# Attention stage: the low part of each weight block by ScalarE's negative high part and an adding transfer, in place of a VectorE subtraction

## The chip, the core and the metric

The kernel runs on one core of a Trainium2 chip. Its engines are TensorE (PE in the profile, PEld for its weight loads), VectorE (DVE), ScalarE (ACT), GpSimd (POOL) and SyncE (SP, which here only starts transfers). Each engine works through its own list of instructions in order, and waits where an instruction's input is not ready. The metric is the device time of one execution in microseconds; of several runs the median is taken.

## The reference, cut to what matters

Two layers over 256 image tokens ("lat") and 256 context tokens ("ctx") of width 1024. Each layer is a half feed-forward, a mixer, and another half feed-forward, each followed by a layer norm. The mixer of the first layer is attention, the only place that the change touches:

```python
def proj(xs):
    p = xs @ w_in                       # 1024 -> 1536 columns
    q, k, v = jnp.split(p, [ATT_HEADS * ATT_HEAD_DIM, (ATT_HEADS + ATT_KV_HEADS) * ATT_HEAD_DIM], axis=-1)
    q = rms_norm(q.reshape(B, L, ATT_HEADS, ATT_HEAD_DIM), q_gain)
    k = rms_norm(k.reshape(B, L, ATT_KV_HEADS, ATT_HEAD_DIM), k_gain)
    ...
s = jnp.einsum('bqhgd,bkhd->bhgqk', q, k).astype(jnp.float32) * (ATT_HEAD_DIM ** -0.5)
p = jax.nn.softmax(s, axis=-1).astype(v.dtype)
...
o_lat = jnp.moveaxis(ob, 0, 1).reshape(B, L, D_MODEL) @ w_out     # 1024 -> 1024
```

Image queries (8 heads) look at all 512 keys, context queries at the 256 context keys; keys and values have 2 heads; image queries and keys are rotated (rope). The mixer's output, times a gate, is added to the residual and normalized.

## The kernel before

**Products in three.** All large products run on TensorE in a rounded float32 type (F32R). To keep float32 accuracy, each operand is held as two tiles: a high part `h` (the value rounded to F32R) and a low part `l` (the value minus `h`). A product is three matmuls into one accumulator, high x high, high x low, low x high (`mm3`, lines 211, 214, 215; `token_product`, lines 726 to 728, where the tokens are the stationary side).

**Weight blocks.** Weights come as blocks of 128 x 1024 float32 (512 KB). `raw` (line 173) takes one of 3 buffers of the tag "raw" and starts the load on SP (line 179). `pair` (line 182) takes one of 7 buffers of the tag "w", which hold a high and a low part. `chunk` (line 187) does both and calls `split`, which makes the parts: ScalarE writes the high part (line 194), VectorE subtracts it from the raw block and writes the low part (line 199). Where `self.fine` is set, as it is throughout attention, VectorE does this in four quarters of 256 columns, so that TensorE can begin with the first; otherwise in one piece. Only when VectorE is done is the raw buffer free for the next load. `split` is also used for everything else that needs two parts: activations, queries, keys, values, probabilities.

`Stream` asks `chunk` for a block when the program first uses it and holds the last block alone; `Keep` holds all its blocks. Buffers of one tag are given out in the order of the program; an instruction that writes a new tile waits until an old tile's last reader has finished.

**Order of the work.** The program is traced in Python order, and a planner then writes each engine's list when the program is built: of what is ready by its own estimates, the instruction that stands first in the program. `pin` keeps some instructions in program order. [...]

**The stage.** `attention` follows the first half feed-forward, whose last products and whose layer norm (`norm`, lines 380 to 480, one generator per token group, advanced by `steps`) still run when it begins. It has these parts:

- `part(blk, tt)`: the input projection, 6 column blocks of 256, each of two weight blocks (12 in all, held with `Keep`), times 4 token tiles of 128. Blocks 0 to 2 for the image tokens, then for the context tokens, then block 3 for all; blocks 4 and 5 follow, partly between the heads.
- `evac` and `turn`: the rms norm of queries and keys (sum of squares on ScalarE, line 782; reciprocal root on VectorE, lines 223 to 234; scaling, line 789), the rotation on GpSimd (lines 752 to 758), and transposes on TensorE (line 797).
- `scores` and `values`: for each head and each of three row blocks the scores, the softmax (lines 820 to 833, one of the three scalings on GpSimd), transposes (line 840), the split of the probabilities, and the product with the values. The probabilities' parts take a buffer of the tag "w" per head.
- `mix_unit`: the output projection, one unit per 128 columns; `w0` (4 weight blocks, `Stream`) for the first four heads, beginning between the last heads' work, then `w1` (4 weight blocks) for the others, first for image tokens, then for context tokens. The sums go on VectorE (line 715).

GpSimd has in this stage the rotation, a third of the softmax scalings, and some sums and differences of the layer norm (lines 417 and 454). It starts no transfers in the kernel before. After the stage the second half feed-forward's weights come through the same "raw" and "w" buffers.

Of the kernel before, what the change touches and what calls it, by code (L numbers as in the profile page):

```python
# [13 lines left out]
AF = mybir.ActivationFunctionType  # L14
ALU = mybir.AluOpType
# [96 lines left out]
class Stream:  # L112


    def __init__(self, b, chunks, sh=0):
        self.b, self.chunks, self.kept = b, chunks, (None, None)
        self.sh = sh if callable(sh) else lambda c: sh
# [24 lines left out]
class Body:  # L142
    def __init__(self, ctx, tc, a, out):
        self.tc, self.nc, self.a, self.out = tc, tc.nc, a, out
        self.n = 0
        self.sp = ctx.enter_context(tc.tile_pool(name="sp", bufs=1))
        self.pp = ctx.enter_context(tc.tile_pool(name="pp", bufs=1, space=PSUM))
        self.later, self.running = [], []
        self.fence = {}
        self.fine = False  # L150

        self.nraw, self.spare = 0, None

# [33 lines left out]
    def chunk(self, src, sh=0):  # L187
        r = self.raw(src)
        h, l = self.pair(sh=sh)
        self.split(r, h, l)  # L190
        return h, l

    def split(self, x, h, l):
# [537 lines left out]
    def attention(self, gate, side):  # L731
        nc, V, S, a = self.nc, self.nc.vector, self.nc.scalar, self.a
        with self.tc.tile_pool(name="att", bufs=1) as gp:
# [131 lines left out]
                    kept.append(hd)  # L865

            wait, kept = [], []

            def turns(left):
                while len(wait) > left:  # L870
                    turn(*wait.pop(0))
# [48 lines left out]
            for gr in both:  # L920
                for d in range(ND - MTAIL, ND):
                    self.mix_unit(g, both, d, w1, gr, d * 4, range(4, 8), True, MTAILSTEP)
            self.steps(ENDSTEP)


    def mlstm(self, gate, side):
# [472 lines left out]
```

## Time and profile before

| What | Value |
|---|---|
| Median of 3 runs | 1699.26 us (1698.13 to 1702.44) |
| Span of the profiled execution | 1693.6 us; the profile gives no time of that execution beside its span |
| Median above the span | 5.7 us |
| Busy, TensorE / VectorE / ScalarE / GpSimd | 1643.8 / 1231.7 / 656.3 / 93.6 us |
| Granted TensorE clock, mean | 0.994 |
| Attention, roughly | 374 to 564 us of the span |

The span is the time from the first to the last instruction of the program in one profiled execution. A row of a group of instructions gives its line, engine and operation, what it writes and reads (buffer numbers left out), its shapes and count, then its busy time and the mean of one in ns, then the idle time of the engine just before these instructions and what ended most of it. A row of a timeline gives start and duration in us, then engine and line; "x4" means that four of a kind are merged, and the brackets give an idle time before it and what ended it. A row of waits reads: who waited, for whom, us in total, times, longest. DVE L199 is the subtraction of `split`, whoever called it.

### The profile page before, as it was taken

To read this page: it belongs to the slowest core of one execution; us is meant where nothing else is said; L and a number is where in the kernel's file an instruction comes from. 1 tells how busy PE (TensorE), PEld (TensorE's weight loads), DVE (VectorE), ACT (ScalarE), POOL (GpSimd) and SP (SyncE) were. 2 spreads that over 40 slices of the span, in tenths; PEclk is the share of its full clock that TensorE was granted. 3 is DMA by queue.
4 is the path that set the end of the run, shared out by engine and by line. 5 is a ranking of instruction groups with operands and counts; after the bars stand their busy time and mean duration, and the time that the engine had idled before them with its cause. 6 is when DMAs were issued, how large, how long until landed. Compare 5 with 4: busy or idle time off the path is not lost.

```text
span 1693.6 us, 24765 instructions
## 1 busy us (share of the span) xinstructions
PE 1643.8 (97%) x9432; PEld 1441.6 (85%) x9432; DVE 1231.7 (73%) x2681; ACT 656.3 (39%) x1125; POOL 93.6 (6%) x114
## 2 busy tenths in 40 slices
PE   7999999999899999999999999999999999999997
PEld 6888888899887898888888998888889878999986
DVE  6799977659988899996334977643335967998687
ACT  5622133215465452212331543213322645556541
POOL 0000000002321100000000100000001001120000
PEclk9999999999999999999999999999999999999999
DMA  9576765412102346774222257642221232337542
GB/s 356 184 230 231 236 210 199 149 62 77 61 2 82 119 136 234 229 244 152 93 94 75 101 179 247 215 144 98 99 100 63 94 125 76 113 125 246 178 168 94
DMA packets 71910, 250.49 MB, mean 148 GB/s; under 512 B 7920, under 2 KB 10480, under 8 KB 71792
## 3 DMA queue, kind: packets, MB, share of 16 engines
q1 hardware_dynamic: 71072, 248.15, 43.1%
q8 instruction: 74, 1.21, 0.3%
q10 hardware_dynamic: 720, 0.76, 0.1%
q14 instruction: 44, 0.36, 0.1%
HBM read 247.83 MB, written 1.05 MB: 147 GB/s over the span
## 4 chain that ended last, share of the span: by engine, by line
PE 83%; DVE 11%; ACT 3%; DMA 2%; issue 1%; POOL 0%; ACTq 0%; DVEq 0%; SPq 0%
PE t L214 23%; PE t L215 23%; PE t L211 23%; PE t L668 4%; DVE t L199 3%; PE t L1165 2%; PE t L726 2%; PE t L728 2%; PE t L727 2%; ACT t L194 1%; PE t L380 1%; DVE t L473 1%; DVE t L400 1%; DVE t L475 1%; DVE t L1201 1%
## 5 line engine op out<-in xcount | busy, mean ns | idle before, releaser
L211 PE MATMUL t<-t,t 128*128 128x512 f32 (+2 forms) x2540 | 856.1, 339 | 10.1 <-ACT t L194 7.5
L214 PE MATMUL t<-t,t 128*128 128x512 f32 (+2 forms) x2540 | 858.5, 339 | 1.8 <-DVE t L475 1.3
L215 PE MATMUL t<-t,t 128*128 128x512 f32 (+2 forms) x2540 | 854.4, 337 | 1.9 <-DVE t L199 1.9
L199 DVE TENSOR_TENSOR t<-t,t 128x256 fp32r<-128x256 f32 (+2 forms) x793 | 494.8, 659 | 196.4 <-ACT t L194 195.8
L194 ACT CAST t<-t 128x1024 fp32r<-128x1024 f32 (+2 forms) x463 | 397.7, 880 | 587.0 <-PE t L215 311.2
L211 PEld LDWEIGHTS t<-t,t 128*128 128x128 f32 x2540 | 476.6, 188 | 65.7 <-ACT t L194 9.8
L214 PEld LDWEIGHTS t<-t,t 128*128 128x128 f32 x2540 | 477.7, 188 | 56.5 <-DVE t L475 2.5
L215 PEld LDWEIGHTS t<-t,t 128*128 128x128 f32 x2540 | 477.5, 188 | 55.3 <-DVE t L199 2.8
L290 DVE SCALAR_TENSOR_TENSOR t<-t,t 128x1024 bf16<-128x1024 f32 x224 | 262.6, 1220 | 15.9 <-DMA t<-in_ada_w 15.4
L522 DVE TENSOR_TENSOR t<-t,t 128x512 f32<-128x512 f32 (+1 forms) x93 | 54.0, 585 | 112.1 <-PE t L215 92.4
L521 ACT ACTIVATE t<-t 128x512 f32<-128x512 f32 (+1 forms) x93 | 47.4, 515 | 196.9 <-PE t L215 195.0
L417 POOL TENSOR_TENSOR t<-t,t 128x256 f32<-128x256 f32 x30 | 23.3, 777 | 1161.4 <-ACT t L407 1159.9
L557 DVE SCALAR_TENSOR_TENSOR t<-t,t,t 128x256 f32<-128x256 f32 x96 | 42.7, 478 | 54.2 <-PE t L215 54.2
L726 PE MATMUL t<-t,t 128*128 128x256 f32 (+1 forms) x256 | 80.4, 316 | 0.0
L728 PE MATMUL t<-t,t 128*128 128x256 f32 (+1 forms) x256 | 79.7, 314 | 0.0
L727 PE MATMUL t<-t,t 128*128 128x256 f32 (+1 forms) x256 | 79.5, 313 | 0.0
L1165 PE MATMUL t<-t,t 128*128 128x512 f32 (+1 forms) x248 | 54.8, 373 | 11.0 <-ACT t L274 5.2
L1165 PEld LDWEIGHTS t<-t,t 128*128 128x128 f32 x248 | 46.4, 220 | 19.0 <-ACT t L274 5.2
L668 PE MATMUL t<-t,t 128*128 128x512 f32 x264 | 60.0, 389 | 0.0
L668 PEld LDWEIGHTS t<-t,t 128*128 128x128 f32 x264 | 49.5, 188 | 10.2
L407 ACT ACTIVATE t<-t 128x256 f32<-128x256 f32 x72 | 26.1, 413 | 68.3 <-DVE t L400 68.3
L726 PEld LDWEIGHTS t<-t,t 128*128 128x128 f32 x256 | 49.6, 194 | 3.1 <-DVE t L789 0.3
(164 smaller groups left out, 1067.6 us busy)
## 6 DMA issues: line engine op xcount, KB each, us to landing
t<-in_ffn_in SPq DMA_DIRECT2D x168, 512.0 KB, 4.0
t<-in_ada_w SPq DMA_DIRECT2D x139, 512.0 KB, 4.2
t<-in_ffn_out SPq DMA_DIRECT2D x66, 512.0 KB, 3.7
t<-in_ffn_last SPq DMA_DIRECT2D x22, 512.0 KB, 3.7
t<-in_att_in SPq DMA_DIRECT2D x12, 512.0 KB, 3.5
t<-in_att_out SPq DMA_DIRECT2D x8, 512.0 KB, 3.9
t<-in_ml_qk SPq DMA_DIRECT2D x8, 512.0 KB, 3.4
t<-in_ml_v SPq DMA_DIRECT2D x8, 512.0 KB, 4.0
```

Source lines behind the costliest of these rows:

```text
L194: self.behind(self.nc.scalar.copy(h, x))
L199: self.behind(self.nc.vector.tensor_tensor(out=ls, in0=xs, in1=hs.bitcast(F32), op=ALU.subtract))
L211: ins = mm(out, wh, xh, start=first, stop=False)
L214: mm(out, wh, xl, start=False, stop=False)
L215: mm(out, wl, xh, start=False, stop=last)
L290: ins = nc.vector.scalar_tensor_tensor(self.tmp().bitcast(BF16), r, 1.0, self.cb[:, v, :], ALU.mult, ALU.mult, accum_out=to)
L522: V.tensor_tensor(out=sl, in0=sl, in1=pu[:, :n], op=ALU.mult)
L668: pin(nc.tensor.matmul(ys[tt][i], gs[g], ws[k][w][:, i * 512 : (i + 1) * 512], start=k == 0 and g == w == 0, stop=k == NF - 1 and g == 1,))
L726: mm(o, self.xh[:, k, c], wh, start=k == 0, stop=False)
L727: mm(o, self.xh[:, k, c], wl, start=False, stop=False)
L728: mm(o, self.xl[:, k, c], wh, start=False, stop=k == ND - 1)
L1165: mm = lambda *k, **kw: pin(nc.tensor.matmul(*k, **kw))
```

## The change

A flag `added`, off at first, is switched on in `attention` just before its first projection and off after its last step. While it is on, `chunk` makes the two parts in another way: ScalarE writes the high part as before, ScalarE then writes the negative of the rounded block into the low part's tile, and GpSimd starts a transfer from the raw block to the low part's tile that adds what it carries to what is there. The low part is then raw minus high, as before. VectorE has no part in it, and the four quarters become one transfer of 512 KB. It concerns 20 blocks: 12 of the input projection and 8 of the output projection. Splits of anything but weight blocks stay as they are, and so do all other stages.

```diff
         self.fine = False
+        self.added = False
...
     def chunk(self, src, sh=0):
         r = self.raw(src)
         h, l = self.pair(sh=sh)
-        self.split(r, h, l)
+        if self.added:
+            S = self.nc.scalar
+            self.behind(S.copy(h, r))
+            self.behind(S.activation(l, r, AF.Copy, scale=-1.0))
+            self.nc.gpsimd.dma_start(l, r, accum_op=ALU.add)
+        else:
+            self.split(r, h, l)
         return h, l
...
             wait, kept = [], []
+            self.added = True
...
             self.steps(ENDSTEP)
+            self.added = False
```

## The prediction

> **What bounds the kernel now.** I read the engines' totals first.
>
> ```profile
> PE 1643.8 (97%) x9432; PEld 1441.6 (85%) x9432; DVE 1231.7 (73%) x2681; ACT 656.3 (39%) x1125; POOL 93.6 (6%) x114
> ```
>
> TensorE (PE) is busy in 97% of the span, so a change pays only where PE stands still or is about to. Next the busy time of each engine in the three stretches of attention (columns: length; busy us and instructions of PE, PEld, DVE, ACT, POOL; granted clock; DMA share; GB/s): the projections, the softmax stretch, the output product.
>
> ```profile
> 374.00:436.00 62.00, 60.06 (x501) 59.13 (x499) 58.33 (x205) 34.78 (x88) 12.65 (x16) 1.00 0.28 91
> 436.00:513.00 77.00, 67.69 (x498) 62.97 (x497) 64.65 (x201) 42.60 (x141) 25.27 (x22) 0.93 0.03 9
> 513.00:553.00 40.00, 36.85 (x208) 31.09 (x207) 33.68 (x86) 20.93 (x40) 3.13 (x2) 1.00 0.32 107
> ```
>
> VectorE (DVE) is full in the first stretch, 58.3 of 62 us, yet PE lacks only 1.9 us there: VectorE is late, but seldom late enough to stop PE. ScalarE (ACT) and GpSimd (POOL) have room everywhere. Then the waits between 370 and 560 us (total us, times, longest), those of PE alone:
>
> ```profile
> PE t L211 <- ACT t L194: 7.5, 7, 2.0
> PE t L797 <- POOL t L758: 2.6, 1, 2.6
> PE t L215 <- DVE t L199: 1.9, 1, 1.9
> PE t L380 <- DVE t L357: 1.1, 1, 1.1
> PE t L380 <- DVE t L443: 0.9, 2, 0.6
> ```
>
> VectorE itself stops PE for 1.9 + 1.1 + 0.9 = 3.9 us in all of attention. The largest item is the high-part cast on ScalarE (line 194), and the edit leaves that cast where it is.
>
> **What is taken away.** Line 199, for the 20 weight blocks of attention (12 of the input projection, 8 of the output), four quarter blocks each:
>
> ```profile
> L199 DVE TENSOR_TENSOR t<-t,t 128x256 fp32r<-128x256 f32 x106 | 41.9, 431 | 8.1 <-ACT t L194 8.1
> L194 ACT CAST t<-t 128x1024 fp32r<-128x1024 f32 x25 | 26.0, 1048 | 28.4 <-PE t L215 19.0 <-DMA t<-in_att_out 3.3 <-PE t L797 3.3
> 535.63 3.43 ACT L194 CAST t<-t 128x512 fp32r<-128x512 f32 x4 [2.59 <-PE t L840]
> ```
>
> That is 80 of the 106 quarter subtractions between 340 and 560 us: 80 x 41.9/106 = 31.6 us of VectorE. What PE can gain from it is less. In the projections the queue on VectorE is long, which one block shows (start, us): its cast, its last quarter's subtraction, and the load that had waited for its raw buffer.
>
> ```profile
> 381.78 1.05 ACT L194 CAST t<-t 128x1024 fp32r<-128x1024 f32 x1 [1.78 <-PE t L215]
> 398.42 0.87 DVE L199 TENSOR_TENSOR t<-t,t 128x256 fp32r<-128x256 f32 x1
> 399.35 29.39 SPq L179 DMA_DIRECT2D t<-in_att_in  x6
> ```
>
> 17.5 us from cast to complete low part; a transfer will be quicker than that, and such loads start earlier. Blocks that VectorE serves at once will be some 5 us later than now, but a block of the projections waits in its buffer for the products of the blocks ahead of it; I price that at nothing, and at 5 us if that cover is gone. The gain is what VectorE's norm chain and sums hold up: 1.1 (line 357) + 0.9 (line 443) = 2.0 us. The 1.9 us before line 215 come from splitting queries, not weights, and the 2.6 us before line 797 from the rotation on GpSimd behind a chain of small VectorE operations; both stay. I count **-2.0 us**; bounds 0 and, with those two, -6.5.
>
> **What is put in.** Per block one more ScalarE pass and one transfer started by GpSimd. The pass has the cast's shape: 1.05 us alone, 0.95 behind another one (the row at 535.63 is a 128x512 cast of 0.59 us and three of 128x1024). 20 x 0.95 = 19 us of ScalarE, which is busy 34.8 of 62 and 20.9 of 40 us in the two stretches where blocks are made: it fits. The transfer, from SBUF to SBUF and adding, has no row here. The nearest:
>
> ```profile
> q1 hardware_dynamic: 71072, 248.15, 43.1%
> t<-in_att_out SPq DMA_DIRECT2D x8, 512.0 KB, 3.9
> t<-in_ml_qk SPq DMA_DIRECT2D x8, 512.0 KB, 3.4
> t<-in_ada_w SPq DMA_DIRECT2D x2, 512.0 KB, 8.7
> 520.42 0.33 SPq L179 DMA_DIRECT2D t<-in_att_out  x1
> L417 POOL TENSOR_TENSOR t<-t,t 128x256 f32<-128x256 f32 x30 | 23.3, 777 | 1161.4 <-ACT t L407 1159.9
> 523.24 1.57 POOL L833 TENSOR_SCALAR t<-t,t 128x512 f32<-128x512 f32 x1 [6.39 <-DVE t L827]
> ```
>
> A load of the same 512 KB lands after 3.9 us; of that, 0.431 x 1693.6 x 0.524/248.15 = 1.5 us is the engines' own time. Adding reads the old block as well, so I count one more such pass: 5.4 us (bounds 3.4, the quickest load, and 8.7, loads in a crowded queue). Starting it costs GpSimd between SP's 0.33 and its own longest operation, 1.57; I take 0.8, its usual one. So a low part is complete 0.95 + 0.8 + 5.4 = **7.15 us** after its cast ends (bounds 4.7 and 11.2).
>
> [...]
>
> **Where it hurts.** The output blocks are made just in time. Rows: for the first two blocks the ScalarE row whose second cast is the block's, for the third the ScalarE row at 535.63 above, then quarter subtractions and PE's first products with each.
>
> ```profile
> 514.69 1.52 ACT L194 CAST t<-t 128x512 fp32r<-128x512 f32 x2
> 518.87 1.09 DVE L199 TENSOR_TENSOR t<-t,t 128x256 fp32r<-128x256 f32 x3
> 519.72 0.39 PE L211 MATMUL t<-t,t 128*128 128x512 f32 x1
> 519.94 0.39 PE L214 MATMUL t<-t,t 128*128 128x512 f32 x1
> 522.85 1.52 ACT L194 CAST t<-t 128x512 fp32r<-128x512 f32 x2
> 526.55 0.40 PE L215 MATMUL t<-t,t 128*128 128x512 f32 x1
> 537.20 3.11 DVE L199 TENSOR_TENSOR t<-t,t 128x256 fp32r<-128x256 f32 x9 [0.25 <-ACT t L194]
> 537.22 0.50 PE L211 MATMUL t<-t,t 128*128 128x512 f32 x1 [1.62 <-ACT t L194]
> 537.79 0.40 PE L215 MATMUL t<-t,t 128*128 128x512 f32 x1
> ```
>
> Each of these casts follows at once on the cast of a head's probabilities (the 128x512 one in its row), and no row of ScalarE names a load that it waited for: the buffers of tag "w" are given out in program order, so a block isn't made sooner unless that head is. The first block's cast ends at 516.2; low part at 523.4; PE needs it at about 519.7: 3.7 us late. The second: 524.4 + 7.15 = 531.5 against 526.55: 5.0 late. The third: cast over by 537.2, so 544.35 against 537.8: 6.6 late. The delays add, because each later cast waits for PE's work behind the earlier stall: **15.3 us** with PE's order as it is (bounds 7.8 and 27.3). (For the third PE waits 1.62 us already.) The subtractions had also come in quarters, so PE could begin on the first; the transfer comes whole.
>
> A planner writes each engine's order when the program is built, and a block that is ready later will be set behind other work. What is there to set before it: the rest of the last two heads,
>
> ```profile
> 518.69 0.28 PE L214 MATMUL t<-t,t 128*128 128x256 f32 x1
> 518.80 0.28 PE L215 MATMUL t<-t,t 128*128 128x256 f32 x1
> 525.81 0.44 PE t L840 x4
> ```
>
> six groups of transposes (0.44 each, by the chain of waits), 2 x 18 products of the values (0.12 from start to start) and the last scores (three products of 512 columns at 0.22, six of 256 at 0.12): 2.6 + 4.3 + 1.4 = 8.3 us. So between 15.3 - 8.3 = 7.0 us and nothing remains (nothing, because heads done earlier also bring the second and third cast forward). I take **+5**, nearer the upper end, because the order is settled before the transfer's real time is known and PE can't change it.
>
> Who else waits: behind each transfer's start on GpSimd stand the rotation (lines 752 to 758) and the scaling of the softmax (line 833), and PE's transposes wait for these; a start that itself waits for ScalarE's second pass holds them up. GpSimd has 3.1 busy us in the last 40, so I add nothing. SP's loads wait for the raw buffer, now returned 7.15 us after the cast, not after 1.5: the third block's cast ends at 537.2, and the load that takes its raw buffer starts at 538.69. The next such load is on the chain of waits already:
>
> ```profile
> 538.69 0.33 SPq L179 DMA_DIRECT2D t<-in_att_out  x1
> 540.03 4.93 DMA t<-in_att_out
> 545.04 1.54 ACT t L194 x2
> ```
>
> That chain would move by 5.6 us; it runs beside the stall on the third block, and counts within the 5.
>
> **Sum.** -2.0 + 5 = +3.0 us. The span is 1693.6 us; the profile gives no separate time of its own execution, and the median of the runs stands 5.7 us above the span, which I carry over unchanged: 1699.3 + 3 = **1702 us**. About 0.3%, 5 us, is what a measurement of this kernel can tell from no change.
>
> **Rivals.** (1) *PE's order stays*: 15.3 - 2.0 = +13.3, **1713** (1705 to 1725 by the bounds). For it: the blocks are tied to the heads by the buffers, and PE works in order. Against: 8.3 us of other work stand ready. (2) *VectorE is what counts*: relieved of 31.6 us, it shortens the chains in front of lines 380, 797 and 215, 6.5 us together, and PE's slow clock in the second stretch (0.93 over 77 us is 5.4 us) halves because PE stops less: -9.2 at best; with 3 us of stall left, -6: **1693**. Place: the projections and the first scores; it decides if the idle time before lines 797 and 215 shrinks below half. Against: VectorE already idles there for ScalarE and GpSimd. (3) *Nothing moves*: the fill hides the latency and VectorE wasn't on the path: **1699**.
>
> [...]
>
> ```profile
> 442.64 1.11 DVE L233 TENSOR_TENSOR t<-t,t 128x4 f32<-128x4 f32 x1
> 444.18 0.16 DVE L233 TENSOR_TENSOR t<-t,t 128x4 f32<-128x4 f32 x1
> 442.47 1.26 POOL L758 TENSOR_TENSOR t<-t,t 128x512 f32<-128x512 f32 x1
> ```
>
> The same operation takes 1.11 us beside GpSimd's rotation and 0.16 us after it. Starts of transfers could do the same to VectorE or suffer it; 20 x 0.95 us, mostly off the path, is within rival 1's range. [...]
>
> **Chances.** Forecast 0.48 (own range 1697 to 1707), rival 1 0.23, rival 2 0.15, rival 3 0.14. Slower by over 0.3%: 0.23 + a third of the forecast, 0.39. Faster: most of rival 2 and a tail of the forecast, 0.17. Within: 0.44. The range runs from just above rival 2's 1693 to rival 1's 1713.
>
> **What would show it.** Right: idle PE before lines 215 between 515 and 560 us, released by a transfer, several us in all; the waits of line 380 on VectorE gone; VectorE some 30 us less busy; transfers that take 3.4 to 8.7 us from start to landing. Wrong: no PE wait on a transfer (then rival 3 or 2); a wait of line 797 that grew (starts in GpSimd's queue); a transfer over 8.7 us, which would also hold up the projections. An order that changed far from attention would upset the sum as a whole.

## The result, and the profile after

The changed kernel takes **1724.2 us** (median of four runs, 1721.9 to 1726.6) against 1698.7 us for the kernel before (four runs, 1698.1 to 1702.4): a ratio of **1.015, interval 1.0133 to 1.0166**. It is 25.5 us slower. The forecast was 1702, its range ended at 1713, so both were wrong, though "slower" held 0.39 of the chance.

The spans of the two profiled executions differ by more, 1723.3 against 1693.6 us: 29.7. The time of a run stands 1.7 to 2.1 us above its span wherever both are known, so the profiled execution of before took some 1695.6 us, about 3 us under its median, and that of after 1725.1, 0.9 us over. What the traces are made to explain is therefore 29.7 us, of which some 4 are chance. Below, a ratio is turned into us with 1698.7.

First the totals of the profile page after: the engines, the queue of GpSimd's transfers (packets, megabytes, share of the span), and the median time of one from issue to landing.

```profile
PE 1655.3 (96%) x9432; PEld 1450.7 (84%) x9432; DVE 1210.2 (70%) x2601; ACT 674.3 (39%) x1145; POOL 109.6 (6%) x134
q0 software_dynamic: 2880, 10.49, 3.3%
t<-t POOLq DMA_DIRECT2D x20, 512.0 KB, 5.3
```

The edit did what it says: 80 operations and 21.5 us fewer on VectorE (31.6 were counted; by the operations' own times the quarters are 32.2 less and all others together 5.2 more, and VectorE's operations overlap by 110.1 us in place of 115.6), 20 passes and 18 us more on ScalarE, 20 transfers of 5.3 us.

Where the time went is read from the busy time by stretch, cut so that both kernels have done nearly the same matmuls at each cut (columns: length; busy us and instructions of PE, PEld, DVE, ACT, POOL; granted clock; DMA share; GB/s). Before:

```profile
366.00:564.00 198.00, 183.50 (x1359) 171.78 (x1357) 169.07 (x521) 106.08 (x277) 42.66 (x42) 0.97 0.20 69
564.00:1694.00 1130.00, 1105.35 (x6464) 973.00 (x6464) 777.08 (x1676) 429.69 (x679) 50.77 (x68) 1.00 0.42 140
```

After:

```profile
366.00:590.00 224.00, 191.25 (x1363) 177.42 (x1362) 148.94 (x446) 122.35 (x296) 57.34 (x61) 0.94 0.42 106
590.00:1723.00 1133.00, 1109.63 (x6464) 976.95 (x6464) 777.12 (x1676) 430.51 (x679) 51.03 (x68) 0.99 0.43 140
```

Attention grew by 26.0 us, everything behind it, up to the ends of the spans, by 3.7 (1129.6 and 1133.3 us). In attention PE stood still for 198.00 - 183.50 = 14.5 us before and for 32.75 after: 18.25 us more. The other 7.75 us are PE busy for longer with some 1360 matmuls in both: the granted clock fell from 0.97 to 0.94, and 0.06 x 224 - 0.03 x 198 = 7.5 us. **So two thirds are stalls and one third is a slower clock.**

What the stalls wait for, between 370 and 600 us after (total us, times, longest):

```profile
ACT t L193 <- DMA t<-in_att_in: 12.2, 3, 7.3
PE t L387 <- DVE t L364: 9.2, 2, 5.2
ACT t L193 <- DMA t<-in_att_out: 8.5, 1, 8.5
PE t L222 <- DMA t<-t: 6.0, 3, 4.4
PE t L804 <- DVE t L240: 3.8, 1, 3.8
PEld t L804 <- POOL t L765: 3.9, 1, 3.9
PE t L222 <- DVE t L206: 2.7, 1, 2.7
PE t L804 <- DVE t L206: 2.0, 1, 2.0
```

(Line 193 is now the high-part cast, 194 ScalarE's second pass, 195 the transfer; other lines have moved down by 7, those from `split` on.) PE's waits for ScalarE's casts, lines 193 and 201, are left out: 8.3 us, 7.5 before. PE's wait for the transfers themselves, line 222, is 6.0 us. The larger part, 9.2 us before line 387 (2.0 before the change) and 5.8 before line 804 (2.6 before), names VectorE, which has less to do than before. The new rows beside them are ScalarE's: its cast waits 20.7 us for weights to arrive, where the row of line 194 before (in the prediction) has 3.3.

How a late load becomes a stall in the layer norm, from GpSimd's and SP's timelines and from the chain of waits of after:

```profile
381.89 0.86 POOL L195 DMA_DIRECT2D t<-t  x1 [3.40 <-PE t L222]
390.14 0.33 SPq L180 DMA_DIRECT2D t<-in_att_in  x1
390.14 5.12 DMA t<-in_att_in
...
395.34 1.04 ACT t L193
396.38 0.42 ACT t L481
...
396.83 0.49 DVE t L482
...
398.10 0.35 DVE t L364
...
398.49 1.24 PE t L387 x2
```

The transfer that starts at 381.89 lands at 390.08 (8.2 us, beside loads). Only then is its raw buffer free, and the load that had waited for it starts at 390.14; in the kernel before, the same load started at 381.74. ScalarE's next instruction is the cast of that block; it stands until 395.34, and behind it in ScalarE's list stands the norm's line 481, which had nothing to do with weights. VectorE and then PE wait for that one: PE stands from 393.31 to 398.49.

This isn't one unlucky block. Nine loads of the projections need a buffer that comes back, and after the change each of the nine starts 0.05 or 0.06 us after a transfer has landed. In the kernel before, six of them started 1.5 to 6.7 us after the end of the cast of the block that had held the buffer, and three, behind VectorE's long queue, 12.8 to 16.5 us after it; now all nine start 5.8 to 10.2 us after it.

The 5.8 us before line 804 come from the last block of the projections. Its load stands behind a transfer until 435.94 (428.41 before the change):

```profile
442.50 1.05 ACT L193 CAST t<-t 128x1024 fp32r<-128x1024 f32 x1 [7.27 <-DMA t<-in_att_in]
445.57 0.17 DVE L230 TENSOR_SCALAR t<-t 128x4 f32<-128x4 f32 x1 [10.38 <-ACT t L789]
449.25 1.26 POOL L759 TENSOR_TENSOR t<-t,t 128x512 f32<-128x512 f32 x1 [3.58 <-DVE t L796]
451.94 1.26 POOL L765 TENSOR_TENSOR t<-t,t 128x512 f32<-128x512 f32 x1
```

While ScalarE stands for that load, the queries' sums of squares (line 789) stand behind it in ScalarE's list. For them wait VectorE's reciprocal root (from line 230) and scaling (line 796), then GpSimd's rotation (lines 759 to 765), then PE's transposes, which start at 453.25. So PE's 3.8 us end with the rotation, as the row of its weight load (PEld) says; line 240 of VectorE only happened to end 0.02 us later. The other 2.0 us, at 446 us, end with VectorE's part of a split whose cast stands behind the same load on ScalarE.

At the end of attention the same happens through SP's list:

```profile
555.37 7.46 DMA t<-in_att_out
...
565.23 4.49 DMA t<-t
569.72 0.02 SPq L180
...
569.77 0.33 SPq L180
...
570.20 9.20 DMA t<-in_c
...
579.47 1.28 ACT L272
...
590.80 0.81 PE t L387 x2
```

A load of weights waits for the raw buffer until 569.72, and SP's next transfer (line 271, an operand of the modulation, 512 KB) waits behind it, takes 9.2 us among the bunched loads (a DMA share of 1.00 from 570 to 580 us, in a row further down), and holds ScalarE until 579.47 and, through the norm, PE until 590.80: 4.05 us of idle PE, 0.9 before. In the kernel before, SP issued the same transfer without such a wait, and it landed in 5 us (SP's and ScalarE's timelines; line 264 is now 271, 265 is 272):

```profile
548.36 0.80 SPq L264 DMA_DIRECT2D t<-in_c  x2
553.47 1.28 ACT L265 ACT_TABLE_LOAD   x1 [2.21 <-DMA t<-in_c]
```

### The profile page after: what moved, and what is told of

It is laid out like the page before. It is cut to its first block, busy times and chain, and to the rows that moved or that the text cites. A ratio compares the mean times of both kernels' runs of the same rounds, so it can differ in the third digit from the quotient of the medians.

```text
span 1723.3 us, 24768 instructions
## 1 busy us (share of the span) xinstructions
PE 1655.3 (96%) x9432; PEld 1450.7 (84%) x9432; DVE 1210.2 (70%) x2601; ACT 674.3 (39%) x1145; POOL 109.6 (6%) x134
## 4 chain that ended last, share of the span: by engine, by line
PE 79%; DVE 11%; DMA 4%; issue 3%; ACT 3%; POOL 0%; SPq 0%; ACTq 0%; DVEq 0%; POOLq 0%
PE t L221 22%; PE t L222 22%; PE t L218 22%; PE t L675 3%; DVE t L206 2%; PE t L1174 2%; PE t L733 1%; PE t L735 1%; PE t L734 1%; PE t L387 1%; ACT t L201 1%; DMA t<-t 1%; DVE t L480 1%; DVE t L407 1%; DVE t L482 1%
## 5 line engine op out<-in xcount | busy, mean ns | idle before, releaser
L206 DVE TENSOR_TENSOR t<-t,t 128x256 fp32r<-128x256 f32 (+2 forms) x713 | 463.3, 684 | 204.7 <-ACT t L201 203.9
L201 ACT CAST t<-t 128x1024 fp32r<-128x1024 f32 (+2 forms) x443 | 377.5, 873 | 573.0 <-PE t L222 292.6
L218 PEld LDWEIGHTS t<-t,t 128*128 128x128 f32 x2540 | 478.7, 189 | 67.1 <-ACT t L201 9.0
L222 PEld LDWEIGHTS t<-t,t 128*128 128x128 f32 x2540 | 480.1, 189 | 63.0 <-DMA t<-t 7.1
L221 PEld LDWEIGHTS t<-t,t 128*128 128x128 f32 x2540 | 479.6, 189 | 57.3 <-DVE t L482 2.5
L733 PE MATMUL t<-t,t 128*128 128x256 f32 (+1 forms) x256 | 81.6, 319 | 0.0
L734 PE MATMUL t<-t,t 128*128 128x256 f32 (+1 forms) x256 | 81.4, 318 | 0.0
L735 PE MATMUL t<-t,t 128*128 128x256 f32 (+1 forms) x256 | 80.8, 316 | 0.0
L1174 PEld LDWEIGHTS t<-t,t 128*128 128x128 f32 x248 | 46.4, 220 | 19.5 <-ACT t L281 4.9
L675 PEld LDWEIGHTS t<-t,t 128*128 128x128 f32 x264 | 49.5, 188 | 10.2
L733 PEld LDWEIGHTS t<-t,t 128*128 128x128 f32 x256 | 50.8, 198 | 2.9 <-DVE t L796 0.3
L734 PEld LDWEIGHTS t<-t,t 128*128 128x128 f32 x256 | 50.9, 199 | 2.7
```

The lines of the kernel that those rows point to most:

```text
L201: self.behind(self.nc.scalar.copy(h, x))
L206: self.behind(self.nc.vector.tensor_tensor(out=ls, in0=xs, in1=hs.bitcast(F32), op=ALU.subtract))
L218: ins = mm(out, wh, xh, start=first, stop=False)
L221: mm(out, wh, xl, start=False, stop=False)
L222: mm(out, wl, xh, start=False, stop=last)
L675: pin(nc.tensor.matmul(ys[tt][i], gs[g], ws[k][w][:, i * 512 : (i + 1) * 512], start=k == 0 and g == w == 0, stop=k == NF - 1 and g == 1,))
```

## The experiments

Theory A: the raw buffer, of which there are three, comes back late, loads come late, and ScalarE, SP and GpSimd, each working through its list in order, stand and hold up work that is not late. Theory B: PE's own waits for late low parts, and what they hand on.

**No transfer at all.** ScalarE's second pass stays, the addition is left out.

```diff
-            self.nc.gpsimd.dma_start(l, r, accum_op=ALU.add)
```

> The changed kernel without the adding transfers; the low part of the 20 weight blocks stays the negative high part, so the output is not the reference's. VectorE is relieved and ScalarE does its second pass, but the raw buffer is free when ScalarE has read it. Theory A (a raw buffer that comes back late delays the next load, and ScalarE's cast that waits for that load holds up what stands behind it) and theory B (TensorE waits for the low parts themselves) both expect 1695 to 1700 us, 0 to 4 us under the kernel before. Theory C (the second pass and the rewritten order cost by themselves) expects 1708 us or more.

Measured 1694.3 us (ten runs), ratio 0.9975 (0.9965 to 0.9985): 4.2 us faster than the kernel before and 0.7 under the range of theories A and B; theory C is out. So VectorE's relief, less whatever ScalarE's 20 passes cost, is worth up to 4.2 us, if nothing comes in its place. (Low parts are sooner here than the change can have them, so this is an upper end.) The transfers cost 25.5 + 4.2, some 30 us.

**The raw buffer held, the low parts as before.** VectorE makes the low parts in the kernel before; GpSimd copies the raw block to a place in DRAM that nobody reads.

```diff
         self.split(r, h, l)
+        if self.added:
+            self.nc.gpsimd.dma_start(self.t([P, 1024], tag="sink", bufs=20, pool=self.dp), r)
```

> The kernel before, with VectorE's subtraction, plus one transfer per weight block of attention, started by GpSimd, that copies the raw block to a scratch in DRAM that nobody reads. Low parts are as early as before; only the raw buffer stays taken until the copy has landed. Theory A expects most of the loss: 1709 to 1718 us, with waits of line 194's cast for loads of 3 us and more. Theory B expects 1699 to 1702 us. Theory C expects about 1700.

Measured 1711.1 us, ratio 1.0078 (1.006 to 1.0095), +13 us, in theory A's range, with PE's order identical to the kernel before. No low part waits for a transfer here, so late raw buffers and a longer GpSimd list cost on their own. But the largest stall is of another kind than in the changed kernel (waits, then GpSimd's timeline):

```profile
PE t L803 <- POOL t L764: 9.0, 1, 9.0
445.08 0.53 POOL L194 DMA_DIRECT2D t<-t  x1 [4.29 <-DMA t<-in_att_out]
445.62 1.27 POOL L758 TENSOR_TENSOR t<-t,t 128x512 f32<-128x512 f32 x1
```

The start of a copy waits for its load on GpSimd, and the rotation (line 758), for which PE waits, stands behind it. In the changed kernel the rotation in front of line 804 is late too, but not behind a start: GpSimd stands idle for VectorE 3.58 us before it (the row at 449.25). The second stall here, 4.9 us before the norm's products at the end of attention, is of the changed kernel's kind. So this run shows that theory A's kind of loss is real, not its size.

**Each half of the change alone.** The flag is taken back before the output blocks (first), or set only there (second).

```diff
                 if MIXAT <= n < MIXAT + ND:
+                    self.added = False      # in the other kernel: True, and not set earlier
```

> The new way for the 12 blocks of the input projection alone; the 8 blocks of the output projection by VectorE as before. Theory A, by the delays read in the changed kernel's trace up to the first scores: about +9 us, 1706 to 1711. Theory B, which has no wait of TensorE for a transfer there: 1697 to 1701.

> The new way for the 8 blocks of the output projection alone. Theory A: the rest of the loss, +14 to +18 us, 1713 to 1717, of which about 7 before the transfer's waiters and the rest at ScalarE's casts and the following norm. Theory B: +8 to +10, 1707 to 1709, all at TensorE's waits for the transfer.

The 12 blocks of the input projection alone: 1707.9 us, ratio 1.0057 (1.0037 to 1.0078), **+9.7 us**, with no PE wait for a transfer. The 8 output blocks alone: 1719.2 us, 1.0119 (1.01 to 1.0138), **+20.2 us**. The first lies in theory A's range, the second above both ranges. In the first the waits are

```profile
ACT t L193 <- DMA t<-in_att_in: 12.6, 3, 6.9
PE t L387 <- DVE t L364: 5.0, 2, 4.1
PE t L804 <- DVE t L240: 3.7, 1, 3.7
```

that is the chain shown above; in the second the two kinds stand side by side:

```profile
PE t L222 <- DMA t<-t: 6.1, 3, 4.5
PE t L387 <- DVE t L364: 5.3, 1, 5.3
```

The sum is 29.9, 4 more than the whole, which is within the three intervals (about 3 us to each side of each).

**A fourth raw buffer, tried too early.** One more buffer, in room that the attention's own pool gives up (the normed queries get two buffers, not three), for the changed kernel, for the kernel before as a control, and for the projection's blocks alone.

```diff
-                q = t([P, n, P], tag="qn", bufs=3)
+                q = t([P, n, P], tag="qn", bufs=2)
...
             self.added = True
+            self.spare = gp
```

> The changed kernel with a fourth raw buffer during attention (the room comes from the normalized queries, two buffers in place of three). Theory A (the loss comes from raw buffers that come back late, which delays loads, and from in-order queues that stand behind the casts that wait for these loads): the waits of ScalarE's casts for loads of the projections and of the output blocks shrink from 7 and 8 us to under 3, and the time falls from 1724 to 1706 to 1713 us, the rest being TensorE's waits for the transfers. Theory B (TensorE waits for the low parts): at most 3 us are won, 1721 to 1724.

> The kernel before with the same fourth raw buffer and two buffers of normalized queries: the control of the run before it. Both theories: 1697 to 1702 us, as before, since no load is waited for long there.

> The new way for the 12 projection blocks alone, with the fourth raw buffer. Theory A: the 9 us of the projections vanish and VectorE's relief shows: 1695 to 1700 us. Theory B makes no difference to the three-buffer version, 1706 to 1710.

All three miss their expectations. The changed kernel takes 1730.4 us (1.0193, 1.0174 to 1.0211) and the projection's blocks alone 1714.7 (1.0099, 1.0081 to 1.0116), both slower than without the buffer; the control takes 1703.6 (1.0028, 1.0018 to 1.0038). The cause lies in the experiment: the buffer's place is free only when the feed-forward's pool ends, and SP starts no load from 361.0 to 391.8 us while it waits for that. PE then waits for projection blocks, which it never did before:

```profile
PE t L734 <- DMA t<-t: 8.8, 3, 5.9
```

So these runs say nothing against theory A or for it. The control gives one thing of use: the room taken from the normed queries costs at most 4.8 us (SP's loads stand still in the control as well), and the wait that goes with it is on GpSimd's rotation, 2.6 us in the kernel before:

```profile
PE t L804 <- POOL t L765: 5.1, 3, 4.0
```

**Four transfers of 256 columns in place of one of 1024**, so that PE can begin with the first.

```diff
-            self.nc.gpsimd.dma_start(l, r, accum_op=ALU.add)
+            for i in range(4):
+                c = slice(i * 256, (i + 1) * 256)
+                self.nc.gpsimd.dma_start(l[:, c], r[:, c], accum_op=ALU.add)
```

> The changed kernel with four adding transfers of 256 columns each per block in place of one. Theory A: the raw buffer comes back after the last of four, some 2.6 us later (three more starts of 0.87 us on GpSimd): slower than 1724, 1726 to 1735 us. Theory B (TensorE could begin with the first quarter, which lands earlier): 1718 to 1724.

1730.1 us, ratio 1.0186 (1.0171 to 1.0202): slower still, as theory A had it.

```profile
t<-t POOLq DMA_DIRECT2D x80, 128.0 KB, 5.0
PE t L224 <- DMA t<-t: 6.3, 5, 2.7
```

(line 224 is here what 222 is in the changed kernel). The median of 5.0 us is one of transfers that run beside each other. Where nothing else moves, the first quarter of a block lands 2.6 to 2.8 us after its start, against 4.4 to 4.6 for a whole block, and the last one, whose start stands behind three others on GpSimd, 5.3 to 5.5 us after the first start. So the block's first quarter is there sooner and its raw buffer comes back later. PE's longest wait fell from 4.4 to 2.7 us, but there are five of them.

**The addend read from DRAM once more.** The raw buffer is then free after ScalarE's second pass, and the low parts are still late. First the whole change, then the projection's 12 blocks alone.

```diff
-            self.nc.gpsimd.dma_start(l, r, accum_op=ALU.add)
+            self.nc.gpsimd.dma_start(l, src, accum_op=ALU.add)
```

> The changed kernel, but the block that the transfer adds is read once more from the weights in DRAM and not from the raw buffer; the low parts are as late as in the changed kernel, the raw buffer is free after ScalarE's second pass, about 2 us after the load. Theory A (the raw buffer that comes back late makes the loads late, and ScalarE and GpSimd stand still behind them): the loads' waits on ScalarE's line 193 fall from 12.2 + 8.5 us to under 5, the stalls before line 387 (5.2 and 4.1 us) and line 804 shrink to about those of the kernel before, and what is left is the wait for the transfers themselves, 6.0 us with some slow clock behind it, on the 1694 of the run without transfers: 1700 to 1708. Theory B (PE's waits for late low parts, and the delays that they hand on, are what costs): nothing changes, 1719 to 1726.

> Only the 12 blocks of the input projection are made by the added transfer, read from the weights in DRAM; the 8 of the output go through VectorE as before. With the raw buffer as source these 12 blocks alone cost 9 us (1707.9), and no PE wait was for a transfer. Theory A: all of the 9 us goes, and some of VectorE's relief is left: 1694 to 1699. Theory B: the low parts are as late as in that run, so 1705 to 1709.

The whole: 1722.1 us, ratio 1.0139 (1.0126 to 1.0152), where theory A had 1700 to 1708; within theory B's range. Yet in the projections theory A's own signs came as it said: the loads' wait on line 193 falls from 12.2 to 1.7 us, the stall at 393 us from 5.2 to 2.3, and the two before line 804 from 5.8 to 0.6 in all. At the output blocks that wait only falls from 8.5 to 6.9, and PE stands longer for the low parts:

```profile
PE t L222 <- DMA t<-in_att_out: 13.6, 2, 9.2
t<-in_att_out POOLq DMA_DIRECT2D x8, 512.0 KB, 10.9
```

An adding transfer from DRAM takes longer: 6.8 to 8.3 us from its start where little else moves, against 4.4 to 4.6 from SBUF, and 10.9 in the median of these eight. PE's waits went from 6.0 to 13.6 us with it, each ending within 0.05 us of a landing. That is theory B measured: what a low part is later, PE stands longer. The run trades one loss for the other, so I had to divide them again.

The projection alone: 1701.0 us (twelve runs), ratio 1.0021 (1.0011 to 1.0031), +3.6 us, against +9.7 from the raw buffer. Between the two expectations, nearer theory A: with transfers that take 8.2 us in the median, two thirds of the loss are gone once the raw buffer is returned early (what the rest is, no run settles). ScalarE's wait shows it, in a trace of the fastest of the twelve runs:

```profile
ACT t L193 <- DMA t<-in_att_in: 0.4, 1, 0.4
```

Here theory B can be excluded as the main cause: the low parts are later than in the run of +9.7.

**The fourth raw buffer, at a time when its place is free:** from the context tokens' projections on, for the whole change; and from the first output block on, with the output blocks alone.

```diff
-                q = t([P, n, P], tag="qn", bufs=3)
+                q = t([P, n, P], tag="qn", bufs=2)
...
                 self.spare = gp      # after the image tokens' blocks 0 to 2; in the other kernel at MIXAT
```

> The changed kernel with a fourth raw buffer, which is used only from the point where the feed-forward's pool is gone, so that its place is free (one buffer of the normed queries is given up for the room). Theory A: one more buffer lets a load start one block earlier, some 10 us, which is more than the 5 to 9 us by which a buffer comes back late: the norm's stalls before line 387 and the waits of ScalarE's line 193 for loads fall by more than half, 1708 to 1718; the waits for the transfers (6.0 us) stay. Theory B: 1721 to 1727.

> Only the 8 output blocks, by the adding transfer from the raw buffer as in the changed kernel, with a fourth raw buffer from the first of these blocks on (one buffer of normed queries fewer for its room, which cost 0.3% in the kernel before). Theory A: the norm's stall of 5.3 us falls below 1, the 6.1 us of waits for transfers stay: 1707 to 1714. Theory B: 1716 to 1721.

1718.7 us (1.0117, 1.0104 to 1.013) and 1714.5 us (1.0086, 1.0067 to 1.0104): +19.9 in place of +25.5, and +14.6 in place of +20.2. Both gain 5.6 us, although both pay for the room (at most 4.8 us by the control; its wait of 4.0 us before line 804 is in both, 4.0 and 3.8); in the second pair the gain is just at the edge of the noise (17.0 to 23.4 us against 11.4 to 17.7). Both times lie just above theory A's ranges, and under theory B's. In the whole, the norm's stall at the end falls from 4.05 to 0.59 us, and ScalarE's wait for loads in the projections from 12.2 to 3.9. Two of theory A's signs did not come: the norm's stall at 393 us, where the buffer is not yet in use, stays at 4.8, and ScalarE's wait for loads of output blocks at 7.8. The waits for transfers stay, 6.1 us in each.

**The output blocks with the raw buffer late and the low parts early.** GpSimd's transfer goes to a place in DRAM that nobody reads; the addition is left out.

```diff
-            self.nc.gpsimd.dma_start(l, r, accum_op=ALU.add)
+            self.nc.gpsimd.dma_start(self.t([P, 1024], tag="sink", bufs=20, pool=self.dp), r)
```

> Only the 8 output blocks are changed; GpSimd's transfer reads the raw buffer as in the changed kernel, but writes to a place in DRAM that nothing reads, so the low part (ScalarE's negative alone, the addition is left out) is there 2 us after the load, while the raw buffer comes back as late as before. With the addition these 8 blocks cost 20.3 us (1719.2). Theory A (the raw buffer): the wait of 8.5 us for a load on line 193 and the norm's stall of 5.3 us before line 387 stay, no PE wait is for a transfer: 1704 to 1711. Theory B (PE's waits for the low parts and what they hand on): 1695 to 1701, because those waits are gone.

1706.5 us (eight runs), ratio 1.0041 (1.0027 to 1.0056), +7.0 us, in theory A's range. No PE wait is for a transfer, and the norm's stall is there:

```profile
PE t L388 <- DVE t L365: 5.6, 1, 5.6
```

(line 388 is 387 of the changed kernel). ScalarE's wait of 8.5 us for a load, which theory A also expected to stay, is 1.5 here, so it hung on more than the buffer (on the late low parts or on the traffic; that isn't divided). A second stall, 6.35 us before its line 805 at 441 us, is GpSimd's rotation behind the start of a copy, as in the second experiment, so the 7.0 holds some of what is the experiment's own.

With that the output blocks' 20.2 us come apart: 7.0 with a late raw buffer alone; 14.6, less up to 4.8 for the room, with late low parts and a buffer to spare. 10 + 7 to 15 + 7, that is 17 to 22, holds the 20.2. **In the output blocks the late low part is the larger cause, in the projections the raw buffer is.**

**Half of the projection's blocks**, those from the context tokens on, from DRAM and from the raw buffer.

```diff
             wait, kept = [], []
-            self.added = True
...
+                self.added = True        # after the image tokens' blocks 0 to 2
...
                 if MIXAT <= n < MIXAT + ND:
+                    self.added = False
```

> Only the last 6 of the 12 blocks of the input projection by the adding transfer, its source the weights in DRAM; everything else by VectorE as before. In the run with all 12 of them the first six cost about 2 us before line 387 (2.3 us of idle PE) and the later ones won back about 4. Theory A: 1694 to 1698, faster than the kernel before by 0.1 to 0.3%. Theory B: 1698 to 1703.

> The same six blocks, with the raw buffer as the source. Theory A: the loads behind them come 3 to 7 us late and ScalarE stands for them, so 3 to 8 us more than the same blocks from DRAM: 1699 to 1705. Theory B: the same as from DRAM within 2 us.

1698.4 us (eleven runs), ratio 0.9997 (0.9987 to 1.0008), and 1700.4 us (eleven), 1.001 (1.0 to 1.002). No version that makes the whole low part beats the kernel before: the best one equals it. The two differ by 2.2 us with intervals that overlap, so they don't decide between the theories. In their traces, from the raw buffer ScalarE waits 4.1 us for one load and PE 3.7 us before line 804; from DRAM PE waits 1.1 there and 1.0 for a transfer.

## Why the prediction was wrong, step by step

**What held.** The second pass is 0.95 us behind the first, a start takes GpSimd 0.86 to 1.0 us (0.8 were taken), a transfer 5.3 us in the median (5.4 were taken, that time counted from issue). The third output block, from the second pass on, with the chain's piece for the transfer:

```profile
549.58 1.06 ACT L194 ACTIVATE t<-t 128x1024 fp32r<-128x1024 f32 x1
550.94 0.87 POOL L195 DMA_DIRECT2D t<-t  x1 [15.48 <-ACT t L194]
550.94 4.38 DMA t<-t
555.36 0.79 PE L222 MATMUL t<-t,t 128*128 128x512 f32 x1 [4.44 <-DMA t<-t]
```

Its cast ended at 549.7, so the low part was there 5.6 us later; 7.15 were reckoned. PE waits for three output blocks as foreseen, for 1.15, 0.45 and 4.44 us: 6.0 in all, against the 5 taken between 7.0 and nothing. That the third was the worst was right too.

The traces also show how 15.3 us became 6.0. PE came to the three low parts 3.5, 2.2 and 0.6 us after the end of the block's cast before the change, and 4.6, 7.1 and 1.2 us after it now: 6.6 us are covered, 4.9 of them at the second block. The low parts were complete 5.7, 7.5 and 5.6 us after the cast, not 7.15: 2.6 us less in all. So work was indeed set in front, though not all of the 8.3 us that I had counted at most. The order changed there: of 9432 matmuls 211 stand in another place, and 63 of these are among 149 places around the output blocks. How much of the 6.6 us is PE's order and how much ScalarE's isn't shown.

**VectorE's relief** was priced at 2.0 us with bounds of 0 and 6.5; without transfers the time falls by 4.2. The wait of 2.6 us before line 797, which I said stays, falls to 0.4 there, as rival 2 had it, while the one of 1.9 before line 215 grows to 3.3. That gain is there and is lost again.

**The step that failed** is the one on buffers: "I price that at nothing, and at 5 us if that cover is gone" for the projection's blocks, and "counts within the 5" for the late loads of the output. I asked when PE needs the low part, and for the projections the answer, in time, was right: PE never waits for one there. For the projections I had read the buffer's return from one block (cast at 381.78, next load at 399.35) and concluded that loads would start earlier. For the three blocks of that kind they start earlier or at the same time (394.01, 399.58 and 403.59 in place of 399.35, 401.90 and 403.57), but for the other six later, by up to 8.4 us (390.14 in place of 381.74). For the output I had seen that the raw buffer comes back 7.15 us after the cast and not 1.5, and followed it to the next load. In neither place did I follow a late load to the instruction that stands first in ScalarE's list, nor to what stands behind it. The cost is 9.7 us in the projections, 6 of it shown to go with the buffer's return, and 5.6 in the output blocks (20.2 less 14.6), or up to 10.4 if the 4.8 for the room come off the 14.6; the run with early low parts had 7.0. Under "Who else waits" I had asked what stands behind a waiting instruction for GpSimd alone, where "I add nothing" was right for the changed kernel (the one PE wait there that ends with GpSimd's rotation, 3.8 us, came from ScalarE's late sums of squares and not from a start), though the copies of two experiments show a stall of 9.0 and one of 6.35 us of that kind.

**The term that was missing** is the clock. Rows of after behind the wait of 4.44 us on the third block (the column before the last two is the granted clock):

```profile
550.00:560.00 10.00, 5.56 (x15) 3.97 (x15) 0.00 (x0) 4.42 (x5) 2.60 (x3) 0.69 0.80 157
560.00:570.00 10.00, 7.72 (x38) 6.36 (x38) 3.04 (x6) 6.76 (x8) 1.74 (x3) 0.84 0.83 223
570.00:580.00 10.00, 10.00 (x63) 8.95 (x62) 4.57 (x11) 2.17 (x3) 0.85 (x1) 0.96 1.00 278
```

3.1 + 1.6 + 0.4 = 5.1 us of clock are lacking in these 30 us. Of that, 0.8 lie in the wait itself (from 550.00 to 555.36 the clock is 0.85), so 4.3 us are lost behind 4.44 + 2.28 = 6.7 us in which PE stands: two thirds as much again. In the run with the output blocks and a spare buffer, the three slices from 540 us on, in which its third block is awaited, show 0.73, 0.84 and 0.74. In the kernel before, all of 500 to 600 us ran at 1.00, so I had no row of it there, but the 0.93 from 436 to 513 stood in my own table, and I used it only for a gain in rival 2. How long PE must stand for the clock to fall, the traces don't settle: 470 to 480 us after shows 0.66 with no idle time longer than 2.7 us near it.

**The sum over again**, in the traces' own us: 6.0 for the transfers, 12.3 for the other stalls, each less what stood there before (18.25 in all), 7.75 of clock, 3.7 behind attention (PE is busy 4.3 us longer there with the same 6464 matmuls): 29.7.

**The rivals.** Rival 1 (order stays, 1705 to 1725) has the right time at its far end for another reason: its 15.3 us of waits for transfers were 6.0. Rival 2's mechanism is true for line 797, not for line 215, and with no transfer in the way it is worth 4.2 us. Rival 3 is out. Whether starts of transfers lengthen VectorE's operations beside them, no run decides. Of the signs named beforehand, some of "right" came (PE idle before line 222 by transfers, transfers within 3.4 to 8.7 us in the median); VectorE is 21.5 us less busy, not 30. But the waits of line 380, now 387, on VectorE did not go: they grew from 2.0 to over 9 us, and that was the sign that a whole path was missing from the sum. Two of the signs of "wrong" came as well: single transfers of 9.2 us, and a wait of line 797, now 804, that grew from 2.8 to 6.0 us, though not by starts in GpSimd's queue, as I had supposed.

## What to carry to other kernels

When an edit makes the reader of a buffer slower, price the buffer's return, not only the result: follow the next load to the instruction that waits for it, and everything that stands behind that one in the same engine's list, whatever it belongs to. Stalls of PE are to be counted together with the clock: here attention lost 7.5 us more of it than before, beside 18.25 us of added stalls, 0.4 of their length, and 4.3 us behind the 6.7 in which PE stands at the third output block and just after it, two thirds. Work that is taken from a full engine is worth only what that engine's rows hold up in PE (4.2 us for the 31.6 counted here), so what replaces it may cost hardly any latency.

## What the runs showed that I had not expected

Transfers and loads that run beside each other take longer: an adding transfer of 512 KB within SBUF lands 4.4 to 4.6 us after its start alone and, in the changed kernel, up to 9.2 beside loads, and loads of 512 KB, 3.4 us in the median of the projection's blocks where only the output's are changed, take 5.1 and 7.5 in the chains shown of after. One of 128 KB lands after 2.6 to 2.8 us alone, but four of them, started one after the other, after 5.3 to 5.5. With the addend from DRAM the transfers of the projection's 12 blocks take 8.2 us in the median, with the raw buffer 5.9, each in the run with these blocks alone. And a start takes the GpSimd engine 0.86 us in the median of the 20 that add, and 0.53 to 0.59 in the rows of those that copy to DRAM.
